# RWKV time mixing: twenty units transposed by DMA instead of eighteen, with a reordered last load, warm-up and tail

## The chip, the core and the metric

The kernel runs on one core of a Trainium2 chip. The core has a matrix engine (TensorE, PE in the profile), a vector engine (VectorE, DVE), a scalar engine (ScalarE, ACT), a general engine (GpSimd, POOL) and an engine that here only issues transfers (SyncE, SP). They run side by side, each through its own list of instructions in order, and wait for one another by semaphores. Sixteen DMA engines move data between HBM and the on-chip memory (SBUF); matmul results land in a smaller memory (PSUM), in banks. The metric is the device time of one execution in microseconds; lower is better.

## What is computed

The input x has 16 batches of 2048 rows of 256 numbers. Each row is mixed with the row before it by per-column weights, and projected:

```python
x_prev[:, 1:, :] = x[:, :-1, :]
xv = x * time_mix_v + x_prev * (1 - time_mix_v)
xr = x * time_mix_r + x_prev * (1 - time_mix_r)
v = xv.reshape(-1, d_model) @ value_weight
r = xr.reshape(-1, d_model) @ receptance_weight
out = (1 / (1 + np.exp(-r)) * v) @ output_weight
```

The reference also computes a key projection, whose result is not used in the output; the kernel leaves it out.

## The kernel before

A batch is cut into four units of 512 rows, so there are 64 units, numbered 0 to 63. For the projections the 256 columns of x must lie on the partitions, so each unit is transposed. In most units TensorE does it (`transposes`, L188: eight 128x128 blocks, L200, evicted by ACT, L216). In the last ones the DMA does it from SBUF to SBUF, called the crossbar here (`by_dma`, L179, issued on SP at L181): two units of batch 11 and then batches 12 to 15 whole, 18 units in all (BYDMA, L55). A transposed batch is kept in a tile `xt` with one slot more than it has blocks: slot 0 holds the last block shifted by one column, so that the row before each row is always one slot to the left. There are three such buffers.

The main loop (L499) runs over units g. In it TensorE does the receptance projection (psum_r, L279), ACT the sigmoid (s_sb, L512), TensorE the value projection (psum_v, L279), DVE their product (z_sb, L549), and TensorE the output projection of an earlier unit (psum_o, L303), which ACT evicts (L335) and SP stores, two units at a time (1 MB, L313). The mixed inputs are made one or two units ahead: a scaling of the slots to the left, by DVE (L249), POOL (L259) or ACT (L491), and an addition by DVE (L271). All this is an order written out by hand: each engine executes what the loop emits for it, in that order.

The order around the change is set by a few constants. CROSS (L56) is 40: from this unit on, the transposed data come by DMA, the output projection falls two units behind instead of one (LATE_O), and half of the scalings move from DVE to ACT (FREE). `advance` (L415) issues loads and TensorE transposes up to six units ahead. A load of a whole batch is one DMA issued by POOL (L109), converting to bf16 on the way; the last one, of batch 15, is issued in unit 34. At L513 unit 40 issues two crossbar transposes for batch 11, which wait until that last load has landed; L517 to L522 issue the other batches, the first in unit 41, and copy slot 0 on ACT (L522), for batches 12 to 15 in units 45, 49, 53 and 57. SP's list has the stores and these transposes in one row, so a waiting transpose holds back the stores behind it.

PSUM has two buffers for transposes (ps_t) and one each for psum_r, psum_v and psum_o. The last four units differ: `output` (L323) evicts units 60 and 61 by halves, one half in ps_t and one in psum_o, and `last_unit` (L347) runs unit 63 by halves, with the two halves of unit 62's output between them, and evicts the last four blocks one at a time.

Before the data arrive, TensorE runs small matmuls on zeros (`warm_up`, L141): 21 at first, and 10 after the first transposes (`first_transposes`, L218), which are evicted to `xt_first`: slot 0 by DVE (L229), the rest by ACT (L230).

Of the kernel before, what the change touches and what calls it, by code (L numbers as in the profile page):

```python
# [8 lines left out]
FP32 = mybir.dt.float32  # L9
BF16 = mybir.dt.bfloat16  # L10
ALU = mybir.AluOpType
# [4 lines left out]
def kernel(  # L16
# [25 lines left out]
    nc = tc.nc  # L42

    B, S, D = x.shape
    P = 128
    KO = D // P
    J = S // P
    UJ = 4
    TU = UJ * P
    UB = J // UJ  # L50
    NU = B * UB
    LOOK = 6
    BYUNIT = 2
    H = UJ // 2
    BYDMA = 4 * UB + 2  # L55
    CROSS = NU - BYDMA - LOOK  # L56
    FREE = CROSS
    LATE_O = CROSS
    START_T = [1, 3, 5, 6, 7, 9, 11, 12]
    AHEAD = 6  # L60
    PAIRS = 10
    WARM = 21
    WARM2 = 10

    consts = ctx.enter_context(tc.tile_pool(name="consts", bufs=1))
    xpool = ctx.enter_context(tc.tile_pool(name="xpool", bufs=6))
# [4 lines left out]
    ps_t_pool = ctx.enter_context(tc.tile_pool(name="ps_t", bufs=2, space=bass.MemoryType.PSUM))  # L71
    ps_v_pool = ctx.enter_context(tc.tile_pool(name="ps_v", bufs=1, space=bass.MemoryType.PSUM))
    ps_r_pool = ctx.enter_context(tc.tile_pool(name="ps_r", bufs=1, space=bass.MemoryType.PSUM))
    ps_o_pool = ctx.enter_context(tc.tile_pool(name="ps_o", bufs=1, space=bass.MemoryType.PSUM))

    ctx.enter_context(tc.manual_schedule())
    SYNC = mybir.DependencyInfo(mybir.DependencyClass.Sync, mybir.DependencyReason.DATA)

    late_copies = []
    x_bf = {}  # L80
    xt = {}
    mix = {}
    o_sb = {}


    zeros = consts.tile([P, P], BF16)
    nc.vector.memset(zeros, 0.0)  # L87
    ident_f = consts.tile([P, P], FP32)
    make_identity(nc, ident_f)
# [3 lines left out]
    def rows(b):  # L93
        return x[b].rearrange("(p j) d -> p j d", p=P)
# [5 lines left out]
    def load(b):  # L100
        if b not in x_bf:
            x_bf[b] = xpool.tile([P, J, D], BF16, name="x_bf")
        if b < BYUNIT:
            for e in range(UB):
                nc.gpsimd.dma_start(
                    out=x_bf[b][:, e * UJ : (e + 1) * UJ, :], in_=unit_rows(x, b, e)[:, 0]
                )
            return
        return nc.gpsimd.dma_start(out=x_bf[b], in_=rows(b), max_dma_last_dim=8192)  # L109

    x_unit = opool.tile([P, 3, UJ, D], FP32, name="o_sb")
    tm_rows = consts.tile([2 * KO, P], FP32)
# [26 lines left out]
    load(2)  # L139

    def warm_up(n):  # L141
        ps = ps_t_pool.tile([P, P], FP32, name="ps_t")
        for _ in range(n):
            nc.tensor.matmul(out=ps, lhsT=zeros, rhs=zeros, start=True, stop=True)  # L144

    warm_up(WARM)

# [31 lines left out]
    def by_dma(b, lo, hi, after=None):  # L179

        op = nc.sync.dma_start_transpose(  # L181
            out=xt[b][:, 1 + lo : 1 + hi].rearrange("p j k c -> p (j k) c"),
            in_=x_bf[b][:, lo:hi].rearrange("p j d -> p (j d)"),
        )
        if after is not None:
            tc.add_manual_dep(op.ins, after.ins.name, SYNC, reason="not beside a load")
# [31 lines left out]
    def first_transposes():  # L218
        def half(h, pool, name):
            ps = pool.tile([P, UJ, KO, P], FP32, name=name)  # L220
            for jj in range(H):
                for ko in range(KO):
                    nc.tensor.transpose(
                        out=ps[:, jj, ko],
                        in_=x_unit[:, 0, h * H + jj, ko * P : (ko + 1) * P],
                        identity=ident_f,
                    )
            if h == 1:
                nc.vector.tensor_copy(out=xt[0][:, 0, :, 1:P], in_=ps[:, H - 1, :, 0 : P - 1])  # L229
            nc.scalar.copy(out=xt[0][:, 1 + h * H : 1 + h * H + H], in_=ps[:, 0:H])  # L230

        half(1, ps_r_pool, "psum_r")
        half(0, ps_v_pool, "psum_v")
# [74 lines left out]
                stop=(ko == KO - 1),  # L308
            )

    def store(queue, b, lo, hi):
        dst = out[b].rearrange("(p j) d -> p j d", p=P)
        queue.dma_start(out=dst[:, lo:hi, :], in_=o_sb[b][:, lo:hi, :])  # L313

    def out_part(pool, name, z, b, e, jj, n, copy, queue):
        ps = pool.tile([P, n, D], FP32, name=name)
        for k in range(n):
            out_matmuls(ps, z, jj + k, k)
        lo = e * UJ + jj
        copy(out=o_sb[b][:, lo : lo + n, :], in_=ps)  # L320
        store(queue, b, lo, lo + n)

    def output(g, z):  # L323
        b, e = divmod(g, UB)
        if e == 0:
            o_sb[b] = opool.tile([P, J, D], FP32, name="o_sb")
        j0 = e * UJ
        if g >= NU - 4:
            for h, (pool, name) in enumerate([(ps_t_pool, "ps_t"), (ps_o_pool, "psum_o")]):
                out_part(pool, name, z, b, e, h * H, H, nc.scalar.copy, nc.sync)  # L330
            return
        ps = ps_o_pool.tile([P, UJ, D], FP32, name="psum_o")
        for jj in range(UJ):
            out_matmuls(ps, z, jj, jj)
        nc.scalar.copy(out=o_sb[b][:, j0 : j0 + UJ, :], in_=ps)  # L335
        if b < BYUNIT:
            if e % 2 == 1:
                nc.sync.dma_start(
                    out=unit_rows(out, b, e - 1, 2),
                    in_=o_sb[b][:, j0 - UJ : j0 + UJ, :].rearrange("p (e j) d -> p e j d", j=UJ),  # L340
                )
        elif g >= NU - 8:
            store(nc.sync, b, j0, j0 + UJ)
        elif e % 2 == 1:
            store(nc.sync, b, j0 - UJ, j0 + UJ)

    def last_unit(g):  # L347


        b, e = divmod(g, UB)  # L350
        s_sb = zpool.tile([P, KO, TU], BF16, name="s_sb")
        z_sb = zpool.tile([P, KO, TU], BF16, name="z_sb")
        cols = [(h * H * P, (h + 1) * H * P) for h in range(2)]
        spare = [(ps_r_pool, "psum_r"), (ps_t_pool, "ps_t"), (ps_v_pool, "psum_v"), (ps_t_pool, "ps_t")]
        banks = [pool.tile([P, KO, H * P], FP32, name=name) for pool, name in spare]

        by_act, by_dve = nc.scalar.copy, nc.vector.tensor_copy
        for h, (lo, hi) in enumerate(cols):
            project(banks[h], g, 0, lo, hi)
            nc.scalar.activation(out=s_sb[:, :, lo:hi], in_=banks[h], func=ACT.Sigmoid)  # L360
        def value(h):
            lo, hi = cols[h]
            project(banks[2 + h], g, 1, lo, hi)
            nc.vector.tensor_tensor(
                out=z_sb[:, :, lo:hi], in0=s_sb[:, :, lo:hi], in1=banks[2 + h], op=ALU.mult
            )

        def before(h):
            pool, name = [(ps_o_pool, "psum_o"), (ps_r_pool, "psum_r")][h]
            out_part(pool, name, z_prev, b, e - 1, h * H, H, by_act, nc.sync)  # L370

        before(0)
        value(0)
        before(1)
        value(1)
        out_part(ps_v_pool, "psum_v", z_sb, b, e, 0, 1, by_act, nc.sync)
        out_part(ps_o_pool, "psum_o", z_sb, b, e, 1, 1, by_dve, nc.sync)
        out_part(ps_t_pool, "ps_t", z_sb, b, e, 2, 1, by_act, nc.scalar)
        out_part(ps_t_pool, "ps_t", z_sb, b, e, 3, 1, by_dve, nc.sync)

# [29 lines left out]
        )  # L410

    tnext = 1
    last_load = None

    def advance(limit):  # L415
        nonlocal tnext, last_load
        while tnext <= min(limit, NU - 1):
            b, e = divmod(tnext, UB)
            if b == 1 and e > 0:
                load(b + e + 1)  # L420
            elif b > 1 and e == 0 and b + 5 < B:
                if b == 2:
                    load(6)
                last_load = load(b + 5)
            if tnext < NU - BYDMA:
                transposes(tnext)
            tnext += 1

    first_transposes()
    for ko in range(KO):  # L430
        nc.vector.tensor_scalar(
            out=w_prev[:, ko, :],
            in0=w_f32[:, 0, ko, :],
# [65 lines left out]
    for g in range(NU - 1):  # L499
# [10 lines left out]
            project(ps_r, g, 0)  # L510
        s_sb = zpool.tile([P, KO, TU], BF16, name="s_sb")
        nc.scalar.activation(out=s_sb, in_=ps_r, func=ACT.Sigmoid)  # L512
        if g == CROSS:  # L513
            for e in (1, 2):
                by_dma(B - 5, e * UJ, (e + 1) * UJ, last_load)
        advance(START_T[g] if g < len(START_T) else g + LOOK - (g == CROSS - 1))
        for b in range(B - 4, B):  # L517
            if g == max(UB * (b - 2) - 1, CROSS + 1):
                new_xt(b)
                by_dma(b, 0, J)  # L520
            if g == UB * (b - 1) + 1:
                nc.scalar.copy(out=xt[b][:, 0, :, 1:P], in_=xt[b][:, J, :, 0 : P - 1])  # L522
        if LATE_O < g < NU - 2:
            output(g - 2, z_prev2)
# [21 lines left out]
            scale_act(pieces(1)[1], (0,))  # L546
            advance(2)
        z_sb = zpool.tile([P, KO, TU], BF16, name="z_sb")
        nc.vector.tensor_tensor(out=z_sb, in0=s_sb, in1=ps_v, op=ALU.mult)  # L549
        for p in pooled[g]:  # L550
            scale_pool(p, last)
        for p in held[g]:
# [37 lines left out]
```

## Time and profile before

| | |
|---|---|
| median of 4 runs | 203.63 us (203.02 to 203.73) |
| the profiled execution | 202.93 us |
| its span, first to last instruction | 201.2 us |
| mean granted TensorE clock | 0.998 |
| TensorE transposes of bf16 data (L200) | 344, 43 units |
| sigmoids (L512), mean of one | 1032 ns |
| PSUM evictions to xt (L216) and to o_sb (L335) | 1029 ns, 1018 ns |
| products z_sb (L549) of a whole unit | 1216 ns |
| the same product of half a unit (L364) | 689 and 686 ns |
| last load (L109), issued | 115.06 us, landed 17.8 us later |
| crossbar transposes (L181) | 6, first issued at 133.00 us |

The span is what lies between the first and the last instruction in the trace; the execution's own time is some 1.7 us longer. A row of the profile names line, engine, operation and tiles, how often it ran, its busy time and the mean of one. In a timeline the first number is the start in microseconds from the span's start and the second the duration. Neighbouring instructions of an engine overlap a little, so their starts can be closer together than their durations. A wait is named by the instruction that ended it; of a queue (SPq, ACTq) it is the wait before a transfer is issued.

### The profile page before, as it was taken

The page shows a single profiled execution, that of the slowest core. Times are in us where ns is not written, and L with a number is a line of the kernel's source. Part 1 is how long each engine was busy: PE and PEld are TensorE (multiplying, and loading weights), DVE is VectorE, ACT ScalarE, POOL GpSimd, SP SyncE. Part 2 cuts the span into 40 slices and gives each one's busy share as a digit, 9 for nine tenths or more (in the row PEclk, how much of TensorE's full clock was granted, in tenths as well). Part 3 has the DMA queues.
Part 4 walks back from the last instruction along what each step waited for, and adds up shares of the span by engine and source line. Part 5 has one row for each costly group of instructions (what it writes and reads, how often), then busy time and mean ns, then how long its engine had stood idle before and what let it go on. Part 6 is the DMA issues. An engine that isn't in the chain of part 4 may idle for free.

```text
span 201.2 us, 3922 instructions
## 1 busy us (share of the span) xinstructions
PE 195.8 (97%) x1436; PEld 126.6 (63%) x1436; DVE 186.6 (93%) x301; ACT 180.7 (90%) x202; POOL 83.4 (41%) x109
## 2 busy tenths in 40 slices
PE   7999999999999999999999999999999999999992
PEld 7675676666666666666666666665656565655671
DVE  2899999999999999999999999999999999999963
ACT  2699899999999999999999999989999999999982
POOL 1744543462542644344462543434344444444200
PEclk9999999999999999999999999999999999999999
DMA  5999999999999999999999999999999999877575
GB/s 168 292 181 217 242 280 275 276 280 277 296 312 311 315 314 301 291 314 298 294 296 288 297 314 297 298 331 223 292 171 404 272 381 178 346 313 314 212 311 210
DMA packets 31130, 56.74 MB, mean 282 GB/s; under 512 B 19716, under 2 KB 21000, under 8 KB 28040
## 3 DMA queue, kind: packets, MB, share of 16 engines
q1 hardware_dynamic: 26160, 40.24, 59.4%
q0 software_dynamic: 4800, 16.12, 40.4%
q8 instruction: 11, 0.18, 0.3%
q10 hardware_dynamic: 152, 0.13, 0.2%
q14 instruction: 7, 0.06, 0.1%
HBM read 34.34 MB, written 33.55 MB: 338 GB/s over the span
## 4 chain that ended last, share of the span: by engine, by line
PE 86%; ACT 5%; DVE 3%; issue 3%; DMA 2%; SPq 0%; DVEq 0%; ACTq 0%
PE psum_v L279 25%; PE psum_o L303 25%; PE psum_r L279 24%; PE ps_t L200 9%; DMA w_f<-n_receptance_weight_dram 2%; ACT s_sb L512 2%; ACT mix L491 1%; ACT o_sb L335 1%; ACT xt L216 1%; PE psum_r L293 1%; DVE mix L271 1%; DVE z_sb L549 1%; DVE mix L249 1%; PE ps_t L303 1%; PE ps_t L279 0%
## 5 line engine op out<-in xcount | busy, mean ns | idle before, releaser
L259 POOL TENSOR_SCALAR mix<-xt,c_sb 128x1024 bf16<-128x1024 bf16 (+1 forms) x55 | 61.0, 1109 | 91.8 <-DVE mix L271 79.5
L549 DVE TENSOR_TENSOR z_sb<-s_sb,psum_v 128x1024 bf16<-128x1024 bf16 x63 | 76.6, 1216 | 3.6 <-PE psum_v L279 1.5
L271 DVE TENSOR_TENSOR mix<-mix,xt 128x1024 bf16<-128x1024 bf16 x112 | 77.2, 697 | 1.7
L279 PEld LDWEIGHTS <-w_bf 128*128 128x128 bf16 x516 | 48.6, 98 | 38.1 <-issue 0.7
L512 ACT ACTIVATE s_sb<-psum_r 128x1024 bf16<-128x1024 f32 x63 | 65.0, 1032 | 3.4 <-PE psum_r L279 2.7
L335 ACT COPY o_sb<-psum_o 128x1024 f32<-128x1024 f32 x60 | 61.1, 1018 | 7.5 <-PE psum_o L303 7.5
L279 PE MATMUL psum_v<-mix,w_bf 128*128 128x512 bf16 (+1 forms) x256 | 65.3, 378 | 0.3 <-DVE z_sb L549 0.2
L303 PE MATMUL psum_o<-wo_bf,z_sb 128*128 128x256 bf16 x494 | 64.4, 273 | 0.1
L279 PE MATMUL psum_r<-mix,w_bf 128*128 128x512 bf16 (+1 forms) x252 | 64.2, 378 | 0.1
L303 PEld LDWEIGHTS <-z_sb 128*128 128x128 bf16 x512 | 49.8, 98 | 20.8 <-issue 1.5
L216 ACT COPY xt<-ps_t 128x1024 bf16<-128x1024 bf16 x38 | 38.7, 1029 | 0.0
L200 PEld LDWEIGHTS <-x_bf 128*128 128x128 bf16 x344 | 22.6, 98 | 9.2 <-POOL xt_first L407 0.2
L200 PE MATMUL ps_t<-ident,x_bf 128*128 128x128 bf16 x344 | 25.8, 219 | 0.0
L249 DVE TENSOR_SCALAR mix<-xt,c_sb 128x1024 bf16<-128x1024 bf16 (+1 forms) x50 | 22.5, 459 | 0.0
L491 ACT ACTIVATE mix<-xt,c_sb 128x1024 bf16<-128x1024 bf16 x11 | 12.7, 1157 | 0.0
L109 POOL DMA_DIRECT2D x_bf<-in_x_dram x14 | 10.5, 749 | 0.0
L271 DVE TENSOR_TENSOR mix<-mix,xt_first 128x1024 bf16<-128x1024 bf16 x15 | 10.2, 684 | 0.1
L259 POOL TENSOR_SCALAR mix<-xt_first,c_sb 128x512 bf16<-128x512 bf16 x6 | 4.1, 685 | 8.1 <-DVE xt_first L408 8.0
L249 DVE TENSOR_SCALAR mix<-xt_first,c_sb 128x512 bf16<-128x512 bf16 x22 | 6.7, 353 | 0.2
L216 ACT COPY xt_first<-ps_t 128x1024 bf16<-128x1024 bf16 x5 | 5.2, 1035 | 0.0
L144 PE MATMUL ps_t<-zeros 128*128 128x128 bf16 x31 | 3.3, 289 | 1.0 <-DVE zeros L87 1.0
L144 PEld LDWEIGHTS <-zeros 128*128 128x128 bf16 x31 | 3.0, 137 | 1.0 <-DVE zeros L87 1.0
(64 smaller groups left out, 48.2 us busy)
## 6 DMA issues: line engine op xcount, KB each, us to landing
out_dram<-o_sb SPq DMA_DIRECT2D x28, 1024.0 KB, 9.4
x_bf<-in_x_dram POOLq DMA_DIRECT2D x14, 1024.0 KB, 27.1
out_dram<-o_sb SPq DMA_DIRECT2D x4, 512.0 KB, 2.7
out_dram<-o_sb SPq DMA_DIRECT2D x6, 256.0 KB, 2.5
x_bf<-in_x_dram POOLq DMA_DIRECT2D x5, 256.0 KB, 6.8
o_sb<-in_x_dram SPq DMA_DIRECT2D x2, 512.0 KB, 5.1
o_sb<-in_x_dram SPq DMA_DIRECT2D x2, 256.0 KB, 2.8
out_dram<-o_sb SPq DMA_DIRECT2D x3, 128.0 KB, 2.0
```

The lines of the kernel that those rows point to most:

```text
L109: return nc.gpsimd.dma_start(out=x_bf[b], in_=rows(b), max_dma_last_dim=8192)
L200: nc.tensor.transpose(out=ps[:, jj], in_=src[:, jj, ko * P : (ko + 1) * P], identity=idn)
L216: nc.scalar.copy(out=xt[b][:, j0 : j0 + UJ], in_=ps)
L249: nc.vector.tensor_scalar(out=mixed(piece)[:, :, ko], in0=xt[b][:, slots(piece), ko], scalar1=c_sb[:, m, ko : ko + 1], scalar2=None, op0=A ...
L259: op = nc.gpsimd.tensor_scalar(out=mixed(piece)[:, :, 1], in0=xt[b][:, slots(piece), 1], scalar1=c_sb[:, m, 1:2], scalar2=1.0, op0=ALU.mul ...
L271: return nc.vector.tensor_tensor(out=mixed(piece), in0=mixed(piece), in1=xt[b][:, slots(piece, 1)], op=ALU.add)
L279: nc.tensor.matmul(out=ps[:, mo, :], lhsT=w_bf[:, m, ko, mo * P : (mo + 1) * P], rhs=mixed((b, m, e * TU + lo, e * TU + hi))[:, :, ko], st ...
L303: nc.tensor.matmul(out=ps[:, slot, :], lhsT=z[:, ko, jj * P : (jj + 1) * P], rhs=wo_bf[:, ko, :], start=(ko == 0), stop=(ko == KO - 1),)
L335: nc.scalar.copy(out=o_sb[b][:, j0 : j0 + UJ, :], in_=ps)
L491: nc.scalar.activation(out=mixed(piece)[:, :, ko], in_=xt[b][:, slots(piece), ko], func=ACT.Copy, scale=c_sb[:, m, ko : ko + 1],)
L512: nc.scalar.activation(out=s_sb, in_=ps_r, func=ACT.Sigmoid)
L549: nc.vector.tensor_tensor(out=z_sb, in0=s_sb, in1=ps_v, op=ALU.mult)
```

## The change

BYDMA goes from 18 to 20, so that batch 11 comes by the crossbar whole, and CROSS from 40 to 38. The load of batch 15 becomes two loads of half a batch each. Two stores, of units 32-33 and 34-35 (`WAITING`), are kept: SP issues the first when the first half of the last load has landed, then four transposes of one unit each for batch 11 when the second half has landed, then the second kept store. The copy of slot 0 for batch 11 is on ACT, in unit 40.

```diff
-    BYDMA = 4 * UB + 2
+    BYDMA = 5 * UB
+    WAITING = range(CROSS - 6, CROSS - 2)
...
-        return nc.gpsimd.dma_start(out=x_bf[b], in_=rows(b), max_dma_last_dim=8192)
+        if b < B - 1:
+            return nc.gpsimd.dma_start(out=x_bf[b], in_=rows(b), max_dma_last_dim=8192)
+        return [
+            nc.gpsimd.dma_start(out=x_bf[b][:, j : j + J // 2], in_=rows(b)[:, j : j + J // 2])
+            for j in (0, J // 2)
+        ]
...
-            store(nc.sync, b, j0 - UJ, j0 + UJ)
+            pair = (b, j0 - UJ, j0 + UJ)
+            if g in WAITING:
+                kept.append(pair)
+            else:
+                store(nc.sync, *pair)
...
-        if g == CROSS:
-            for e in (1, 2):
-                by_dma(B - 5, e * UJ, (e + 1) * UJ, last_load)
...
-        for b in range(B - 4, B):
-            if g == max(UB * (b - 2) - 1, CROSS + 1):
+        for b in range(B - 5, B):
+            if g == max(UB * (b - 2) - 1, CROSS + 3 * (b > B - 5)):
                 new_xt(b)
-                by_dma(b, 0, J)
-            if g == UB * (b - 1) + 1:
+                if b == B - 5:
+                    store(nc.sync, *kept.pop(0), after=half_load)
+                    for e in (3, 0, 1, 2):
+                        by_dma(b, e * UJ, (e + 1) * UJ, last_load)
+                else:
+                    by_dma(b, 0, J)
+                if kept:
+                    store(nc.sync, *kept.pop(0))
+            if g == UB * (b - 1) + (b > B - 5):
                 nc.scalar.copy(out=xt[b][:, 0, :, 1:P], in_=xt[b][:, J, :, 0 : P - 1])
```

At the start, the warm-up matmuls are fewer and have 512 columns instead of 128 (5 for 21, and 3 for 10; the tile of zeros grows to match), and ACT's eviction of the second half of unit 0 comes before DVE's copy of its slot 0 instead of after it.

```diff
-    WARM = 21
-    WARM2 = 10
+    WARM = 5
+    WARM2 = 3
...
-    zeros = consts.tile([P, P], BF16)
+    zeros = consts.tile([P, TU], BF16)
...
+            nc.scalar.copy(out=xt[0][:, 1 + h * H : 1 + h * H + H], in_=ps[:, 0:H])
             if h == 1:
                 nc.vector.tensor_copy(out=xt[0][:, 0, :, 1:P], in_=ps[:, H - 1, :, 0 : P - 1])
-            nc.scalar.copy(out=xt[0][:, 1 + h * H : 1 + h * H + H], in_=ps[:, 0:H])
```

In the tail, both halves of the outputs of units 60 and 61 go to ps_t, and the product of unit 62 is made in two halves. In `last_unit` the halves of the receptance projection and of unit 62's output now alternate, the first of these outputs is evicted by DVE instead of ACT, the second half of unit 63's product is made a block at a time, and the second of the four last blocks is evicted by ACT instead of DVE.

```diff
-            for h, (pool, name) in enumerate([(ps_t_pool, "ps_t"), (ps_o_pool, "psum_o")]):
-                out_part(pool, name, z, b, e, h * H, H, nc.scalar.copy, nc.sync)
+            for h in range(2):
+                out_part(ps_t_pool, "ps_t", z, b, e, h * H, H, nc.scalar.copy, nc.sync)
...
-        before(0)
-        value(0)
-        before(1)
-        value(1)
+        receptance(0)
+        out_part(ps_o_pool, "psum_o", z_prev, b, e - 1, 0, H, by_dve, nc.sync)
+        receptance(1)
+        value(0, H)
+        out_part(ps_r_pool, "psum_r", z_prev, b, e - 1, H, H, by_act, nc.sync)
+        value(1, 1)
         out_part(ps_v_pool, "psum_v", z_sb, b, e, 0, 1, by_act, nc.sync)
-        out_part(ps_o_pool, "psum_o", z_sb, b, e, 1, 1, by_dve, nc.sync)
+        out_part(ps_o_pool, "psum_o", z_sb, b, e, 1, 1, by_act, nc.sync)
...
-        nc.vector.tensor_tensor(out=z_sb, in0=s_sb, in1=ps_v, op=ALU.mult)
+        n = TU // 2 if g == NU - 2 else TU
+        for c in range(0, TU, n):
+            nc.vector.tensor_tensor(
+                out=z_sb[:, :, c : c + n],
+                in0=s_sb[:, :, c : c + n],
+                in1=ps_v[:, :, c : c + n],
+                op=ALU.mult,
+            )
```

More of the change, by code (lines that the diff above doesn't have):

```diff
@@ L79 @@
     late_copies = []
+    kept = []
     x_bf = {}
@@ L141, in warm_up @@
     def warm_up(n):
-        ps = ps_t_pool.tile([P, P], FP32, name="ps_t")
+        ps = ps_t_pool.tile([P, TU], FP32, name="ps_t")
         for _ in range(n):
-            nc.tensor.matmul(out=ps, lhsT=zeros, rhs=zeros, start=True, stop=True)
+            nc.tensor.matmul(out=ps, lhsT=zeros[:, 0:P], rhs=zeros, start=True, stop=True)
     warm_up(WARM)
@@ L309, in out_matmuls, with store @@
             )
-    def store(queue, b, lo, hi):
+    def store(queue, b, lo, hi, after=None):
         dst = out[b].rearrange("(p j) d -> p j d", p=P)
-        queue.dma_start(out=dst[:, lo:hi, :], in_=o_sb[b][:, lo:hi, :])
+        op = queue.dma_start(out=dst[:, lo:hi, :], in_=o_sb[b][:, lo:hi, :])
+        if after is not None:
+            tc.add_manual_dep(op.ins, after.ins.name, SYNC, reason="in turn with the last load")
     def out_part(pool, name, z, b, e, jj, n, copy, queue):
@@ L357, in last_unit, with receptance, value @@
         by_act, by_dve = nc.scalar.copy, nc.vector.tensor_copy
-        for h, (lo, hi) in enumerate(cols):
+        def receptance(h):
+            lo, hi = cols[h]
             project(banks[h], g, 0, lo, hi)
             nc.scalar.activation(out=s_sb[:, :, lo:hi], in_=banks[h], func=ACT.Sigmoid)
-        def value(h):
+        def value(h, n):
             lo, hi = cols[h]
             project(banks[2 + h], g, 1, lo, hi)
[L364 to L370, printed above, removed]
-        before(0)
-        value(0)
-        before(1)
-        value(1)
+            for c in range(lo, hi, n * P):
+                nc.vector.tensor_tensor(
+                    out=z_sb[:, :, c : c + n * P],
+                    in0=s_sb[:, :, c : c + n * P],
+                    in1=banks[2 + h][:, :, c - lo : c - lo + n * P],
+                    op=ALU.mult,
[6 more added lines that the diff above has]
+        value(1, 1)
         out_part(ps_v_pool, "psum_v", z_sb, b, e, 0, 1, by_act, nc.sync)
-        out_part(ps_o_pool, "psum_o", z_sb, b, e, 1, 1, by_dve, nc.sync)
+        out_part(ps_o_pool, "psum_o", z_sb, b, e, 1, 1, by_act, nc.sync)
         out_part(ps_t_pool, "ps_t", z_sb, b, e, 2, 1, by_act, nc.scalar)
@@ L412 @@
     tnext = 1
-    last_load = None
+    half_load = last_load = None
     def advance(limit):
-        nonlocal tnext, last_load
+        nonlocal tnext, half_load, last_load
         while tnext <= min(limit, NU - 1):
@@ L424, in advance @@
                 last_load = load(b + 5)
+                if b + 5 == B - 1:
+                    half_load, last_load = last_load
             if tnext < NU - BYDMA:
@@ L548 @@
         z_sb = zpool.tile([P, KO, TU], BF16, name="z_sb")
-        nc.vector.tensor_tensor(out=z_sb, in0=s_sb, in1=ps_v, op=ALU.mult)
+        n = TU // 2 if g == NU - 2 else TU
+        for c in range(0, TU, n):
+            nc.vector.tensor_tensor(
+                out=z_sb[:, :, c : c + n],
+                in0=s_sb[:, :, c : c + n],
+                in1=ps_v[:, :, c : c + n],
+                op=ALU.mult,
+            )
         for p in pooled[g]:
```

## The prediction

> **What bounds the kernel now.** The page comes first: TensorE is busy 97% of the span, and the chain of waits runs through it for 86%.
>
> ```profile
> span 201.2 us, 3922 instructions
> ...
> PE 195.8 (97%) x1436; PEld 126.6 (63%) x1436; DVE 186.6 (93%) x301; ACT 180.7 (90%) x202; POOL 83.4 (41%) x109
> ...
> PE 86%; ACT 5%; DVE 3%; issue 3%; DMA 2%; SPq 0%; DVEq 0%; ACTq 0%
> ```
>
> ACT (90%) and DVE (93%) are so close behind that a share of the span decides nothing; I read the pace. In the timeline of ACT each sigmoid (L512) marks one unit. These are units 37 to 40, then 43 and 45:
>
> ```profile
> 124.58 1.03 ACT L512 ACTIVATE s_sb<-psum_r 128x1024 bf16<-128x1024 f32 x1
> ...
> 127.62 1.03 ACT L512 ACTIVATE s_sb<-psum_r 128x1024 bf16<-128x1024 f32 x1
> ...
> 130.67 1.03 ACT L512 ACTIVATE s_sb<-psum_r 128x1024 bf16<-128x1024 f32 x1
> ...
> 133.27 1.03 ACT L512 ACTIVATE s_sb<-psum_r 128x1024 bf16<-128x1024 f32 x1
> ...
> 141.14 1.01 ACT L512 ACTIVATE s_sb<-psum_r 128x1024 bf16<-128x1024 f32 x1
> ...
> 146.37 1.02 ACT L512 ACTIVATE s_sb<-psum_r 128x1024 bf16<-128x1024 f32 x1
> 147.28 0.41 ACT L522 COPY xt<-xt 128x254 bf16<-128x254 bf16 x1
> 147.57 1.03 ACT L335 COPY o_sb<-psum_o 128x1024 f32<-128x1024 f32 x1
> ```
>
> A unit with TensorE transposes takes 3.05 us (124.58 to 127.62); one without takes 2.60 (130.67 to 133.27), and (146.37 - 141.14)/2 = 2.62 later on. Both are the sum of the matmuls: 0.86 + 0.86 + 0.87, plus 0.45 for eight transposes. The last two rows show ACT without slack: L522 waits for a whole crossbar batch, and the eviction L335 behind it holds back the next output matmul.
>
> Third, the SP queue and the DMA. The queue's waits and its timeline say when the crossbar could begin; the queue tables of five windows give the rates (packets, MB, share): loads alone (16 to 20 us), loads and stores together (112.5 to 124.7, two rows), crossbar alone (136 to 140.8), stores alone (152.2 to 155.2).
>
> ```profile
> SPq L181 <- DMA x_bf<-in_x_dram: 1.7, 1, 1.7
> ```
>
> ```profile
> q0 software_dynamic: 257, 0.86, 108.6%
> ```
>
> ```profile
> q0 software_dynamic: 395, 1.49, 60.4%
> q1 hardware_dynamic: 294, 2.15, 43.5%
> ```
>
> ```profile
> q1 hardware_dynamic: 4179, 1.05, 113.2%
> ```
>
> ```profile
> q1 hardware_dynamic: 175, 1.30, 102.9%
> ```
>
> Loads alone run at 0.215 MB/us, beside stores at 0.122. A 1.05 MB batch takes the crossbar 4.8 us (1.2 a unit), a store 2.4 us.
>
> **Part 1, two more units by the crossbar.** TensorE loses 16 transposes: 2 x (3.05 - 2.62) = **-0.86 us**. ACT loses two evictions (L216, 1.03 each), and gains one scaling (L491, 1.16, moved from DVE, where it was 0.48) and one copy of slot 0 (L522, 0.41; as a DVE copy it was 0.22). The steps of units 40 to 43 now come at 38 to 41, which is a pattern that the trace already has; only the copy at unit 40 is new in it.
>
> A rule speaks against this. The Trainium skill, "VectorE: DVE Perf Modes", section "The three transpose paths", has a 128x128 block at 390 ns on TensorE and 1309 ns by the crossbar, and its rules prefer TensorE where PSUM will do. By these the 16 blocks would lose 16 x 0.92 = 14.7 us if they lay on the path. The trace's rows are 0.45/8 = 0.056 us a block on TensorE, and 4.8/32 = 0.15 on the crossbar, beside TensorE and not on it. I take the rows: it is TensorE's time that is scarce.
>
> **Part 2, when the crossbar can start.** The times below are in the time of before, less what TensorE has gained by then. Before: the last load was issued at 115.06 and landed at 132.9, and SP waited the last 1.7 us for it. From 118.6 on the load queue still had 1.50 MB to move (sum over windows). Now the stores of units 32-33 (issued 118.6 before) and 34-35 (124.7) stand back. The store before them landed at 121.7: some 2 us at 0.12, then 1.27/0.215 = 5.9 us alone, so 126.6. Before, most had arrived at 131 while the last engine's share landed at 132.9; with 1 to 2 us of such spread the load lands near **128.2**, and its first half near 125.5. The kept store issued then has 2.4 us of packets, from about 127.0 to 129.4, mostly behind the load and not beside it. It is SP's only business there, so nothing else waits behind it.
>
> Transposes issue from 128.2, 1.37 us each on SP (two rows of 1.40 and 1.31). The first landed 3.8 us after issue before: now 132.0. Who waits: ACT's slot-0 copy in unit 40, ready at 133.1 (sigmoid 138.27 - 6.09 + 0.92). Margin 1.1 us. (6.09 is the shift of the pattern: unit 40's sigmoid stood at 133.27, unit 38's will stand at 124.58 + 2.60 = 127.18.) Behind that copy on ACT stand the eviction of unit 38, the scaling and the next sigmoid, and TensorE waits for both of them: a late landing costs TensorE about 1:1. The copy itself adds 0.29 us in a unit that already has the scaling; the same place before had 0.3 us of slack, so I take +0.05 (0 to +0.3). POOL needs the third transpose at 136.3; it lands at 134.7.
>
> **Part 3, what queues behind.** SP must then issue the second kept store, the store of units 36-37 and the whole batch 12, in this order. The crossbar ends its four units at 134.4, two stores take it to 139.5 with their start, batch 12 to 144.4, landing about 1 us later: **145.4**. Before it landed at 143.4. Its reader is L522 of unit 45, now at 147.28 - 0.86 = 146.4. Margin 1.0 us, where it was 3.9. Here a second rule counts: "DMA: Bandwidth & Descriptors", section "Latency and other measured facts", gives a DMA transpose 261 GB/s effective; this trace has 1.05 MB in 4.8 us, 219 GB/s, and later batches were slower (landing after 10.4 and 11.5 us, a store before them included). By the page two batches' worth of packets end 1.6 us sooner and the margin is 2.6; by the trace it is 1.0, and with a batch of 6.5 us it is -0.7. I keep the trace. Later batches have about 6 us of slack before and 2 or more now. The output buffers of batch 8, stored late, are next written by unit 44's eviction near 148; their store lands near 138.
>
> **Part 4, the tail.** Before, the second half of unit 60's output waited for psum_o, which the eviction of unit 59 held (189.44 to 190.46):
>
> ```profile
> 189.81 0.60 PE L303 MATMUL ps_t<-wo_bf,z_sb 128*128 128x256 bf16 x4
> 190.51 0.60 PE L303 MATMUL psum_o<-wo_bf,z_sb 128*128 128x256 bf16 x4
> ```
>
> Both halves in ps_t: -0.27. Then unit 62's product starts at 192.82 instead of 193.06, and its first half (0.69 instead of 1.22) frees the output matmuls at 193.5. Following TensorE, ACT and DVE row by row (matmul blocks 0.43, halves on ACT 0.59, DVE halves 0.69, quarters 0.42; the half eviction on DVE, not in the trace, lies between 0.42 for 256 columns and 0.84 for twice that, taken as 0.69), the last DVE eviction ends at 197.7 instead of 198.26, ACT's last at 197.35 instead of 197.99. The extra instruction of each split product (about 0.16) is inside this. **-0.55** (-0.8 to +0.1).
>
> **Part 5, the start.** The larger memset costs 0.15 more (0.112 for 64 words, 0.06 for one, so 0.8 ns a word); five warm-ups of four times the columns take as long as 21, and TensorE has 0.30 us free before L162. The three later ones end near 6.3, before L293 at 6.38. ACT's copy goes 0.08 earlier, DVE's w_prev 0.1 later. Cover: the transposes of unit 1 waited 0.49 us for their load, at 7.40, whatever went before. 0 (-0.1 to +0.3; the upper end if all three run at the slow pace of 0.107 per 128 columns).
>
> **Sum.** -0.86 + 0.05 - 0.55 + 0 = **-1.35 us**. The profiled execution took 202.93 (span 201.2), so it would take 201.6. It lies 0.7 under the median of the runs (203.63), from which I subtract the same: **202.3**. A measurement tells 0.3%, 0.6 us, from no change.
>
> **Rivals.**
> A, as summed: 202.3, by itself 201.6 to 202.9. Chance 0.46.
> B, the wait moves to batch 12: L522 of unit 45 waits 0.5 to 1.3 us. For it: the slow batches, and SP's order with two stores in front; against: the margin of 1.0. With 0.7 us from a 6.5 us batch: 203.0. Chance 0.22.
> C, slower: the last load doesn't land sooner, because the skew of its engines decides and not the store traffic, or because the kept store runs beside its second half. Needed is 133.1 - 3.8 = 129.3; the whole gain is used up at 130.7, and from 131.3 the kernel is measurably slower. At 132.9, as before, ACT waits 3.6 us in unit 40: 203.63 - 1.35 + 3.6 = 205.9; halfway, 204.3. Against it: TensorE's side is sure, and loads alone did run at 0.215. Chance 0.22.
> D, the tail gives nothing, since the last stores' landing sets the end or another wait fills in: 202.8. Chance 0.10.
>
> Faster: A, most of D and a third of B, 0.61. Same: the rest of B and a little of D, 0.17. Slower: C, 0.22. The range 201.6 to 204.3 takes in A, B, D and the milder half of C.
>
> **What would show it.** Right: sigmoids 2.6 us apart from unit 37 on except one step of 2.9; SP's wait for the load ending near 128; no wait of L522's successor on a DMA in units 40 and 45; the last eviction about 1.4 us earlier. Wrong: an ACT idle stretch released by the xt transposes, a load landing past 130, or a start of L293 after 6.5.

## The result, and the profile after

The changed kernel takes **204.36 us** (median of 31 runs, 203.60 to 205.34), the kernel before 203.45 beside it (50 runs): ratio 1.0039, 95% interval 1.0027 to 1.0050. In a second comparison an unaltered copy took 204.39 against 203.74: 1.0031 (1.0011 to 1.0052). The change makes the kernel slower by 0.3 to 0.4%, 0.7 to 0.9 us; 202.3 had been predicted.

The page of the profile after:

```profile
span 203.2 us, 3851 instructions
...
PE 195.2 (96%) x1397; PEld 123.8 (61%) x1397; DVE 186.8 (92%) x301; ACT 180.2 (89%) x202; POOL 83.8 (41%) x110
...
PE 77%; DVE 9%; issue 4%; DMA 3%; ACT 2%; SPq 1%; POOL 0%; DVEq 0%
```

TensorE has 39 matmuls and 39 weight loads less (1436 to 1397 each) and works 0.6 us less, yet the span is 2.0 us longer. So the time is lost where TensorE is idle. The timeline of ACT shows that it is not lost in the units that the crossbar part of the change touches: the sigmoids (now L532) of units 37 to 40, 43 and 45, and then the two rows at the margin of batch 12.

```profile
126.27 1.03 ACT L532 ACTIVATE s_sb<-psum_r 128x1024 bf16<-128x1024 f32 x1
...
128.87 1.03 ACT L532 ACTIVATE s_sb<-psum_r 128x1024 bf16<-128x1024 f32 x1
...
131.73 1.03 ACT L532 ACTIVATE s_sb<-psum_r 128x1024 bf16<-128x1024 f32 x1
133.88 1.02 ACT L532 ACTIVATE s_sb<-psum_r 128x1024 bf16<-128x1024 f32 x1 [0.21 <-PE psum_r L286]
...
142.06 1.02 ACT L532 ACTIVATE s_sb<-psum_r 128x1024 bf16<-128x1024 f32 x1
147.29 1.02 ACT L532 ACTIVATE s_sb<-psum_r 128x1024 bf16<-128x1024 f32 x1
148.19 0.41 ACT L546 COPY xt<-xt 128x254 bf16<-128x254 bf16 x1
148.48 1.03 ACT L344 COPY o_sb<-psum_o 128x1024 f32<-128x1024 f32 x1
```

From unit 37 on a step takes 2.6 on average (2.60, 2.86 and 2.15 for the first three, 2.61 from unit 43 to 45), and no row is preceded by a wait for a transfer. In the queue of SP the wait for the last load is there once, as foreseen:

```profile
SPq L188 <- DMA x_bf<-in_x_dram: 2.1, 1, 2.1
```

It ended at 128.1; the first crossbar transpose (issued at 128.3) landed at 131.7, batch 12 at 147.0.

What is different lies behind the last unit. The next lines are the last in the answers for the store's line (L320 after, L313 before), for the last six stores, from 196 us on after and from 195 on before: the time from issue to landing.

```profile
DMA to landing us min/median/max: 2.9/3.0/3.8
```

```profile
DMA to landing us min/median/max: 1.9/2.0/2.1
```

A store needs 3.0 us where it needed 2.0. Each store has sixteen reports of arrival in the records, read here as one for each DMA engine, and has landed with the last of them. Of the last store alone: in the profile of before fifteen engines had reported at 200.21 and the sixteenth at 200.23; after, fifteen at 200.84 and the sixteenth at **201.71**. One DMA engine is 0.87 late. The queue tables of that time show what is new there. First after, 195.6 to 197.2 us; then before, 188.2 to 189.4 us, and before from 195 to 201 us (packets, MB, share of 16 engines):

```profile
q1 hardware_dynamic: 301, 0.56, 91.6%
q8 instruction: 1, 0.02, 5.2%
```

```profile
q1 hardware_dynamic: 90, 0.37, 75.3%
q8 instruction: 1, 0.02, 4.6%
```

```profile
q1 hardware_dynamic: 965, 1.35, 61.3%
q10 hardware_dynamic: 144, 0.13, 6.3%
```

Queue 8 carries **instructions**: one packet of 16 KB, on one engine, for 0.052 x 16 x 1.6 = 1.33 us. By the records such a packet comes once per about 250 instructions of TensorE (222 to 276 lie between two), eleven times in either kernel; that the packets are TensorE's is borne out below, where added TensorE instructions move them. In the kernel before the last one ran at 188.34, and none ran while the last stores were moving. With 78 instructions fewer ahead of it, the last one falls at 195.70 in the changed kernel. From then on each store has fifteen reports together and one late, by 1.9 us at the store issued at 194.57 and still by 0.87 at the last, as if the shares on one engine lined up behind the packet. The records don't name the engine of a packet or of a report, so that the two are the same is inferred.

The whole account, of two profiles of each kernel (a second one was taken of both, see below); the landings and SP's closing steps are read from the records of the trace:

| stretch | before, us | after, us | difference of means |
|---|---|---|---|
| start to sigmoid of unit 1 | 12.00, 13.01 | 13.42, 13.30 | +0.85 |
| to sigmoid of unit 37 | 112.58, 112.88 | 112.85, 112.84 | +0.12 |
| to sigmoid of unit 61 | 63.95, 63.96 | 63.18, 63.16 | **-0.79** |
| to end of DVE's last eviction | 9.73, 9.73 | 9.30, 9.31 | **-0.43** |
| to landing of the last store on 15 engines | 1.95, 1.94 | 2.09, 2.09 | +0.15 |
| to landing on the sixteenth | 0.02, 0.02 | 0.87, 0.76 | **+0.80** |
| to SP's first closing step | 0.08, 0.08 | 0.45, 0.45 | **+0.37** |
| to the end of the span | 0.84, 0.86 | 1.05, 1.05 | +0.20 |

Compute gained 1.2 us in the units and the tail, and 1.5 were lost after the last eviction. Of this, 0.15 comes with the new tail: fifteen engines land 2.08 to 2.14 us after the last eviction in the eight profiles of kernels that have it, 1.94 to 2.02 in five of the six others. The third row from below is put down to the instruction packet. The next one is of another kind: SP's and ACT's transfers use eight semaphores in turn, and at the end SP waits for the eight in a fixed order, some 0.06 us each. Before (56 transfers), the last store's semaphore was the last in turn; with two more the turn has moved on, the last store has the second one, and six waits follow its landing. The steps of SP (L616 after, L585 before) from just ahead of that landing to the end of the span:

```profile
L616 SPq EVENT_SEMAPHORE  x9: 17/28/28, 201.7 to 203.1; - x9
```

```profile
L585 SPq EVENT_SEMAPHORE  x3: 17/17/28, 200.2 to 201.1; - x3
```

Two of each row are steps that all engines take together at the end; the others are the waits, seven and one, the last store's own among them.

The first row is not the change's alone. Without it the account makes the changed kernel 0.42 us slower, where the medians of the timed runs have 0.65 and 0.91. The profile of before had an early start, matched by only one of the thirteen others; the transposes of unit 1 wait for their rows:

```profile
7.40 1.10 PE L200 MATMUL ps_t<-ident_f,o_sb 128*128 128x128 f32 x8
```

```profile
8.82 0.88 PE L207 MATMUL ps_t<-ident_f,o_sb 128*128 128x128 f32 x6 [1.28 <-DMA o_sb<-in_x_dram]
```

The load was issued at 2.15 us in both. The second profile of the same kernel before had this:

```profile
8.41 1.10 PE L200 MATMUL ps_t<-ident_f,o_sb 128*128 128x128 f32 x8 [0.73 <-DMA o_sb<-in_x_dram]
```

### The profile page after: what moved, and what is told of

Same layout as the page of the kernel before. It is cut to its first block, busy times and chain, and to the rows that moved or that the text cites. A ratio compares the mean times of both kernels' runs of the same rounds, so it can differ in the third digit from the quotient of the medians.

```text
span 203.2 us, 3851 instructions
## 1 busy us (share of the span) xinstructions
PE 195.2 (96%) x1397; PEld 123.8 (61%) x1397; DVE 186.8 (92%) x301; ACT 180.2 (89%) x202; POOL 83.8 (41%) x110
## 4 chain that ended last, share of the span: by engine, by line
PE 77%; DVE 9%; issue 4%; DMA 3%; ACT 2%; SPq 1%; POOL 0%; DVEq 0%
PE psum_v L286 23%; PE psum_o L310 23%; PE psum_r L286 22%; PE ps_t L207 7%; DVE mix L278 4%; DMA o_sb<-in_x_dram 3%; DVE mix L256 3%; DVE z_sb L575 1%; PE ps_t L310 1%; ACT s_sb L532 1%; ACT mix L511 1%; DVE xt_first L426 1%; ACT xt L223 1%; PE psum_r L300 0%; PE ps_t L286 0%
## 5 line engine op out<-in xcount | busy, mean ns | idle before, releaser
L575 DVE TENSOR_TENSOR z_sb<-s_sb,psum_v 128x1024 bf16<-128x1024 bf16 (+1 forms) x64 | 76.8, 1201 | 3.3 <-PE psum_v L286 1.5
L532 ACT ACTIVATE s_sb<-psum_r 128x1024 bf16<-128x1024 f32 x63 | 64.9, 1031 | 3.5 <-PE psum_r L286 2.9
L310 PE MATMUL psum_o<-wo_bf,z_sb 128*128 128x256 bf16 x486 | 63.2, 272 | 0.0
L223 ACT COPY xt<-ps_t 128x1024 bf16<-128x1024 bf16 x36 | 36.5, 1027 | 0.0
L207 PEld LDWEIGHTS <-x_bf 128*128 128x128 bf16 x328 | 21.5, 98 | 8.8
L207 PE MATMUL ps_t<-ident,x_bf 128*128 128x128 bf16 x328 | 24.5, 219 | 0.0
L511 ACT ACTIVATE mix<-xt,c_sb 128x1024 bf16<-128x1024 bf16 x12 | 13.9, 1158 | 0.0
L112 POOL DMA_DIRECT2D x_bf<-in_x_dram x13 | 9.8, 753 | 0.0
L151 PE MATMUL ps_t<-zeros 128*128 128x512 bf16 x8 | 3.6, 606 | 1.2 <-DVE zeros L89 1.2
L216 ACT CAST xt_first<-ps_t 128x512 bf16<-128x512 f32 x4 | 2.1, 588 | 2.9 <-PE ps_t L207 2.9
```

Of the source, the lines that this page charges most:

```text
L207: nc.tensor.transpose(out=ps[:, jj], in_=src[:, jj, ko * P : (ko + 1) * P], identity=idn)
L223: nc.scalar.copy(out=xt[b][:, j0 : j0 + UJ], in_=ps)
L310: nc.tensor.matmul(out=ps[:, slot, :], lhsT=z[:, ko, jj * P : (jj + 1) * P], rhs=wo_bf[:, ko, :], start=(ko == 0), stop=(ko == KO - 1),)
L511: nc.scalar.activation(out=mixed(piece)[:, :, ko], in_=xt[b][:, slots(piece), ko], func=ACT.Copy, scale=c_sb[:, m, ko : ko + 1],)
L575: nc.vector.tensor_tensor(out=z_sb[:, :, c : c + n], in0=s_sb[:, :, c : c + n], in1=ps_v[:, :, c : c + n], op=ALU.mult,)
```

## The experiments

The theory to be tested: the last instruction packet of TensorE, shifted into the last stores, and the order of the closing waits eat the gain. The rivals: the long warm-ups cost time at the start; the two parts (crossbar, tail) are themselves worth nothing; or the crossbar disturbs something later. All ratios are to the kernel before, run beside it, with 95% intervals.

**TensorE instructions put back elsewhere.** The changed kernel, with the projections of three units (20 to 22) in halves: 48 more TensorE instructions far from both ends, and the same columns.

```diff
+    HALVED = range(20, 23)
...
+        if g in HALVED and hi - lo == TU:
+            for mo in range(KO):
+                for c in (0, TU // 2):
...
+                            out=ps[:, mo, c : c + TU // 2],
...
+            return
```

> The changed kernel with the projections of units 20 to 22 in halves of 256 columns: 48 more TensorE instructions at about no time (0.04 us), everything else as it is. Theory 1 (the last 16 KB instruction fetch for TensorE, at 195.7 us in the profile of the changed kernel, holds up one DMA engine's share of the last stores): the fetch moves some 3.9 us earlier, to about 192, the last stores' landings draw together again, and the kernel becomes 1.0 to 1.3 us faster than the changed kernel, so 0.1 to 0.4 us faster than before (ratio to before 0.998 to 0.9995). Theory 2 (the loss is at the start: late first loads or the longer warm-ups): no change, ratio to before 1.004.

Measured: **0.9997** (0.9970 to 1.0024), median 203.68. The last packet came at 191.63; the last store landed on fifteen engines at 200.52 and on the sixteenth at 200.53. Landing of the last stores:

```profile
DMA to landing us min/median/max: 1.9/2.1/2.2
```

A kernel with more to execute is faster by 0.4% than the changed kernel, with its warm-ups and all else the same. Nothing but the late engine distinguishes the two from unit 61 on: the last eviction (9.30 us after the sigmoid of unit 61) and the closing waits (0.45) are the same. Its middle, units 37 to 61, is 0.2 us longer; Part 3 of the section on the prediction says why.

**The same put into the kernel before.** Units 20 to 29 halved, 160 instructions more, which bring a twelfth packet into the tail.

```diff
+    HALVED = range(20, 30)
```

> The kernel before with the projections of units 20 to 29 in halves of 256 columns: 160 more TensorE instructions, about 0.1 us of TensorE time. Theory 1: a twelfth instruction fetch appears some 40 instructions before the end, near 196 to 197 us, and the last stores of one DMA engine land over 1 us after the others: slower by 1.0 to 1.4 us (ratio 1.005 to 1.007). Theory 2: slower by 0.1 us at most (ratio 1.000 to 1.001).

Measured: **1.0074** (1.0050 to 1.0099). The twelfth packet ran at 197.56, and stores landed late again:

```profile
DMA to landing us min/median/max: 2.5/2.8/3.1
```

From the sigmoid of unit 1 to the end this profile took 190.5, against 189.15 and 189.47. The added instructions themselves cost nothing that shows: from unit 1 to unit 37, with the halved units, it took 112.83, against 112.58 and 112.88. The rest is 0.4 more from the last eviction until fifteen engines had reported (half of it because SP issued the last store 0.24 instead of 0.03 after the eviction), 0.35 for the sixteenth, and 0.33 in units 41 to 45, which is not the packet's and which I didn't follow up. The direction is as the packet has it; the size is not all its own.

**The long warm-ups alone.**

```diff
-    WARM = 21
-    WARM2 = 10
+    WARM = 5
+    WARM2 = 3
...
```

> The kernel before with the change's warm-ups alone (5 and 3 of 512 columns, larger tile of zeros): 46 fewer TensorE instructions. Theory 1: the last fetch moves from 188.3 to about 192 and still ends before the last stores: within 0.3 us of before at the end; the start costs at most 0.15. Theory 2: the warm-ups cost what the changed kernel lost at its start, 0.5 to 1.4 us (ratio 1.003 to 1.007), with the full clock granted at about 6.35 us instead of 5.64 and the first mixed matmuls later.

Measured: 1.0006 (0.9985 to 1.0028). In its profile unit 1 started at 8.91, the last packet, at 193.22, took 1.98 us, and the sixteenth engine was 0.71 late, although the packet had ended 4.6 us ahead of the last eviction, where theory 1 expected no delay; together that made a span of 203.4, 2.2 over the first one of before, of which the median shows next to nothing. A single profile measures neither the start nor this packet; I come back to it below.

**The changed kernel with the old warm-ups.** The same edit turned round.

> The changed kernel with the warm-ups of before (21 and 10 of 128 columns): 46 more TensorE instructions. Both theories expect it faster than the changed kernel, theory 1 by 1.0 to 1.3 us and equal to the padded changed kernel within 0.2, theory 2 by 0.5 to 1.4 and faster than the padded one by as much. If both hold, it is the fastest: 1.2 to 1.7 us under the changed kernel, ratio to before 0.995 to 0.998.

Measured: **0.9992** (0.9965 to 1.0018). The last packet is at 191.42; the last store lands on all engines at 199.86. With 46 instructions back, it comes out like the padded kernel, 0.4 to 0.5% under the changed one. The wins of crossbar and tail begin to show, and 0.45 us of closing waits remain.

**The crossbar alone, and the tail alone**, each with the old warm-ups:

```diff
-    BYDMA = 4 * UB + 2
+    BYDMA = 5 * UB
...
```

> The kernel before with the crossbar part of the change alone (20 units, halved last load, kept stores; warm-ups, first transposes and tail as before). The middle, from the sigmoid of unit 37 to that of unit 61, becomes 0.77 us shorter (63.95 to 63.2). The last instruction fetch comes near 191 and delays no last store. But two more transfers on the hardware queues shift the closing checks: the last store's semaphore is checked early instead of last, and some seven checks of 0.06 us follow its landing: +0.4 us after the last landing. Sum: 0.2 to 0.5 us faster than before (ratio 0.9975 to 0.999). The rival, that the crossbar itself gives its gain back, expects 0.9995 to 1.002 and a middle as long as before.

```diff
-            for h, (pool, name) in enumerate([(ps_t_pool, "ps_t"), (ps_o_pool, "psum_o")]):
-                out_part(pool, name, z, b, e, h * H, H, nc.scalar.copy, nc.sync)
+            for h in range(2):
+                out_part(ps_t_pool, "ps_t", z, b, e, h * H, H, nc.scalar.copy, nc.sync)
...
```

> The kernel before with the tail of the change alone. Sigmoid of unit 61 to the last eviction: 0.43 to 0.54 us shorter (9.73 to 9.3 on DVE); fetch at 188.3 and closing checks as before, so the span gains the same: ratio 0.9975 to 0.9985. The rival, that the last stores' landing sets the end whatever the evictions do, expects the landing no earlier and a ratio of 1.000.

Measured: the crossbar 0.9985 (0.9964 to 1.0007), the tail 0.9984 (0.9965 to 1.0003). Both point down by 0.3 us; neither is told from no change by itself. In their profiles the sizes are plain: sigmoids of units 37 to 61 in 63.18 with the crossbar, against 63.95; unit 61 to the last eviction in 9.30 with the tail, against 9.73. The crossbar's kernel has the closing waits of 0.45 too, which takes half of its gain; the tail's kernel has 0.08, but a sixteenth engine 0.23 late and a slower landing by 0.17.

**Two transfers fewer.** Batch 11 goes in two transposes instead of four, of one unit and of three, so that the turn of the semaphores is as before. Once with the old warm-ups and once with the long ones.

```diff
-                    for e in (3, 0, 1, 2):
-                        by_dma(b, e * UJ, (e + 1) * UJ, last_load)
+                    for e, n in ((3, 1), (0, 3)):
+                        by_dma(b, e * UJ, (e + n) * UJ, last_load)
```

> The changed kernel with the warm-ups of before and batch 11's transposes in two transfers (one unit, then three) instead of four: two hardware transfers fewer, so that the last store's semaphore is again the last one checked. If the order of the checks costs what the profiles show, the time from the last landing to SP's first closing step falls from 0.4 to 0.1 us, and the kernel is 0.3 to 0.4 us faster than the changed kernel with the old warm-ups: ratio to before 0.996 to 0.998. If the transposes in one piece of three units make POOL or ACT wait in unit 40 or 41, it gives back up to 1 us.

> The changed kernel with batch 11's transposes in two transfers, and its own warm-ups: the instruction fetch stays in the tail near 195.7. The closing checks end 0.1 instead of 0.4 us after the last landing: 0.3 to 0.4 us faster than the changed kernel (ratio to before 1.002 to 1.003), with one DMA engine's last landings still about 0.9 us after the others.

Measured: **0.9966** (0.9946 to 0.9986) with the old warm-ups, median 203.07: faster than the kernel before and, by the ratios, than the changed one. With the long ones 1.0009 (0.9990 to 1.0027). In the latter the packet stayed at 195.83 and the sixteenth engine was 0.74 late, but SP's first closing step followed the landing by 0.09 instead of 0.45, and the end followed that by 0.84 instead of 1.05. In both kernels the middle, units 37 to 61, took 63.3 to 63.4 us instead of 63.2, as the expectation had held possible; most of this is in the step of unit 43 (2.55 and 2.53 us, where it was 2.37), whose cause is not shown. The four kernels with crossbar and tail form a square:

| | four transposes | two transposes |
|---|---|---|
| long warm-ups | 1.0039 and 1.0031 | 1.0009 |
| old warm-ups | 0.9992 and 0.9989 | 0.9966 |

Each column falls by 0.43 to 0.45%, each row by 0.24 to 0.26%. The account above has 0.80 us (0.39%) for the packet and 0.57 us (0.28%) for the closing steps. By these medians the two add up, but in each row the intervals of the kernels touch or overlap: the timed runs alone hardly show the second effect. It rests on the profiles, where the 0.45 stands in all six with 58 hardware transfers and 0.08 or 0.09 in all eight with 56.

**The start, once more.** In the first ten profiles the kernels with long warm-ups had started unit 1 later than all the others, so four kernels were run again, unaltered.

> The changed kernel unaltered, once more, to read its start. Unit 1's rows landed at 8.8 us in its first profile, and at 7.4 in that of the kernel before; over all profiles the kernels with long warm-ups had 8.2 to 8.9 (four), those with short ones 7.4 to 8.1 (six). Theory 1 (the landing of the first loads differs from run to run, whatever the code): the transposes of unit 1 start anywhere between 7.4 and 8.9, and profiled time less start is as in the first profile, 196.2 within 0.3. Theory 2 (long warm-ups delay them): 8.2 or later again. Both: ratio 1.004 within 0.002, and the last instruction fetch of TensorE at 195 to 196 us beside the last stores.

> The kernel before with the long warm-ups, once more, to read its start. Theory 1: transposes of unit 1 anywhere between 7.4 and 8.9, ratio 1.000 to 1.003. Theory 2: 8.2 or later, and a ratio of 1.003 or more, since 0.8 us later is 0.4%.

> The changed kernel with the old short warm-ups, once more, beside the unaltered one on the same chip. Theory 1: start anywhere between 7.4 and 8.9; ratio 0.997 to 1.001, 0.4% under that of the changed kernel, of which the place of the last instruction fetch is the cause and not the start. Theory 2: start 7.4 to 8.1 again, and profiled time less start no better than in the changed kernel by more than the fetch's 0.85 us and the checks' part.

> The kernel before unaltered, once more, to read its start and as a measure of what a comparison of a kernel with itself gives. Theory 1: start anywhere between 7.4 and 8.9, likely later than the 7.4 of the first profile, with a profiled time later by as much. Theory 2: 7.4 to 8.1. Both: ratio 1.000 within 0.002.

Measured, with the start of unit 1's transposes in the new profile: changed kernel 1.0031 (1.0011 to 1.0052), 8.70; long warm-ups alone 1.0018 (0.9996 to 1.0040), 9.21; old warm-ups 0.9989 (0.9968 to 1.0010), 8.65; kernel before 1.0003 (0.9981 to 1.0026), 8.41. The changed kernel with the old warm-ups:

```profile
8.65 1.09 PE L207 MATMUL ps_t<-ident_f,o_sb 128*128 128x128 f32 x8 [0.89 <-DMA o_sb<-in_x_dram]
```

So a late landing of these rows comes without long warm-ups as well, and the same code gave 7.40 and 8.41. The changed kernel with the old warm-ups started as late as the changed kernel and was 0.9 us shorter in its profile (span 202.0 against 203.0), 0.7 of it behind the last eviction: its packet was at 190.56, the sixteenth engine 0.01 late. But over all profiles the six starts with long warm-ups (8.2 to 9.2) still lie above most of the eight with short ones (7.4 to 8.65). One of the six was late for another reason: in the second profile of the long warm-ups alone the matmuls of unit 0 ran at half pace, for the full clock was granted at 10.05 us only (4.4 to 7.4 in all others), and unit 1 started at 9.21 though its rows had landed at 8.01. There the last of the first transposes had also waited 0.6 us for a load, so that the long warm-ups held the clock back is not shown.

```profile
7.51 1.06 PE L293 MATMUL psum_r<-xt_first,w_prev 128*128 128x512 bf16 x2
8.36 1.06 PE L293 MATMUL psum_r<-xt_first,w_bf 128*128 128x512 bf16 x2
9.21 1.01 PE L200 MATMUL ps_t<-ident_f,o_sb 128*128 128x128 f32 x4
```

What the timed runs allow is small: 1.0006 and 1.0018 for the long warm-ups alone, 0.1 to 0.4 us. The padded kernel says the same: with the long warm-ups but an early packet its ratio is 0.9997, against 0.9992 and 0.9989 with the old ones. Whether a late start or the late engine of the first of these profiles makes up that remainder stays open.

## Why the prediction was wrong

**Part 1** held: -0.86 + 0.05 predicted, -0.79 measured between the sigmoids of units 37 and 61.

**Part 2** held: the load's two halves landed at 125.6 and 128.1 (125.5 and 128.2 predicted), the first transpose at 131.7 (132.0). That the times agree so closely is in part luck, since this profile ran 1.7 us later than the forecast's clock (the sigmoid of unit 37 at 126.27, where 124.58 was taken): the load was issued so much later and took 11.4 us, where 13.1 was put. ACT's copy in unit 40 came 3.1 us after the transpose it needs, not 1.1; over the eight profiles with the crossbar part this margin is 0.2 to 3.1 us and never a wait. Rival C is excluded.

**Part 3** held for the changed kernel: batch 12 landed 1.2 us before ACT's copy at 148.19, where a margin of 1.0 had been put (1.0 in the second profile). Rival B is excluded there, but only just. Batch 12 lands at 146.5 to 147.8 us in all eight profiles with the crossbar part, whether compute runs early or late, and the changed kernel's late start makes room for it. In two profiles that started earlier ACT's copy of unit 45 waited for it: the padded kernel (landed at 147.81, copy at 147.83; 0.2 us lost) and the fastest kernel (146.83 and 146.86; 0.1 us). So rival B is what comes next where the start gets faster.

**Part 4** held in what it worked out. TensorE, ACT and DVE came as followed row by row: with both halves of unit 60 in ps_t they are one group, and the step from the sigmoid of unit 61 to that of unit 62 fell from 3.48 to 3.21, by the 0.27 that was put. The rows below are that group, the product of unit 62 in halves, and the end of compute.

```profile
190.73 1.04 PE L310 MATMUL ps_t<-wo_bf,z_sb 128*128 128x256 bf16 x8
```

```profile
193.72 0.69 DVE L575 TENSOR_TENSOR z_sb<-s_sb,psum_v 128x512 bf16<-128x512 bf16 x1 [0.30 <-ACT s_sb L532]
```

```profile
198.33 0.42 DVE L329 COPY o_sb<-ps_t 128x256 f32<-128x256 f32 x1 [0.49 <-PE ps_t L310]
```

The last evictions gained 0.43 on DVE and 0.54 on ACT, from unit 61 on, where 0.55 was taken. DVE's is the later one, and 0.15 of its 0.43 went in the slower landing.

**The step that failed** is the line "Sum", and behind it the end of Part 4: the sum ends with the last eviction and lets all that comes after it move along unchanged. From there to the end of the span the kernel before takes 2.9 us, the changed one 4.4 (4.46 and 4.35). Rival D named the place ("the last stores' landing sets the end") but only as a gain of nothing; the loss is 0.15 + 0.80 + 0.37 + 0.20 = 1.5 us, more than the whole gain of -1.35. No rival had both: an end set by transfers, and a change that makes these transfers later.

Two of the omissions could have been seen in the profile of before. Parts 1 and 5 counted the 78 removed TensorE instructions by their time and not by their number; the instruction queue stood in the page, and its last packet at 188.34 with one about every 250 instructions put the shift near the tail (78 of 250 is a third of a packet's distance). What a packet costs there, that profile did not show. And the change's two more transfers on SP's queue were costed by their bytes and issue time, and not by the turn that they shift in the closing waits. The 0.20 in the last row of the account has no cause shown: it is there in all five profiles where the new tail and four transposes come together, and absent with either alone. In these five DVE's last closing step starts 0.39 us after ACT's, in the nine others 0.02 to 0.03.

**Part 5** stays near its range: 0.1 to 0.4 us for the long warm-ups by the timed runs, -0.1 to +0.3 predicted. Its sign of being wrong, the first matmuls of unit 0 later than 6.5, came (6.52 and 6.67), but says little: the kernel before had 6.38 and 6.56. Its cover, the wait for unit 1's rows, was read from one profile, whose start no other of fourteen profiles beats. That probably accounts for the 0.7 us by which that profile lay under the median; the prediction carried it along as a constant, which did no harm to the sum, but a direct comparison of the first two spans shows 2.0 us for a change of 0.7 to 0.9.

## What to carry to other kernels

Where the end of a kernel is a string of stores, follow the path past the last eviction: to the landing on the slowest DMA engine, and to the closing waits. A change in the number of instructions moves the instruction packets, and a change in the number of transfers moves the turn of the semaphores; both could be cheaply moved back here, with 48 needless instructions in the middle or two transfers joined. Of a start, take several profiles before a wait in it is counted as cover.

## What the hardware showed that was not expected

- TensorE's instructions arrive during the run as single packets of 16 KB, about one per 250 instructions, in 0.9 to 2.0 us each. With one of these beside the last stores, one of their sixteen shares came up to 1.9 us late. Its place is not all that counts: of seven packets that began 6.3 to 7.8 us ahead of the end of the last eviction, one (the slowest, 1.98 us) went with a last store 0.7 us late, and six with 0.02 or less.
- SP's closing waits are serial, about 0.06 us each; their order relative to the last store was worth 0.37 us in the profiles, without any change in the stores.
- The load of unit 1's rows, issued at 2.15 to 2.17 us, landed between 7.36 and 8.86 us over fourteen profiles, and the full clock was granted between 4.4 and 10.05 us.
- Batch 12, whose transfer stands behind the last load, landed at 146.5 to 147.8 us in eight profiles whose compute lay up to 1.6 us apart.
